# Strassen's block products in the second feed-forward stages of a two-layer decoder trunk

## The chip, the cores and the metric

The kernel runs on one core of one Trainium2 chip. The metric is device microseconds for one execution. Before the change the median of three runs is 1214.55 us (1214.17 to 1214.58).

## What is computed

A decoder trunk of two layers on a sequence of 256 rows and 1024 columns, in fp32. Each layer has a feed-forward half-step, a mixer (a state-space group beside differential attention), a cross attention into 256 memory rows, and a second feed-forward half-step. Cut to what matters here:

```python
D_MODEL = 1024; SEQ = 256; DEPTH = 2
D_FF = ((8 * D_MODEL // 3 + 127) // 128) * 128          # 2816

def rms_norm(x, gain):
    y = x * lax.rsqrt(jnp.mean(x * x, axis=-1, keepdims=True) + EPS)
    return y * gain

def swiglu(x, w_gate, w_up, w_down):
    return (jax.nn.silu(x @ w_gate) * (x @ w_up)) @ w_down

h = x
for l in range(DEPTH):
    h = h + 0.5 * swiglu(rms_norm(h, ffn1_norm[l]), ffn1_w_gate[l], ffn1_w_up[l], ffn1_w_down[l])
    h = h + hybrid_mixer(rms_norm(h, mix_norm[l]), ...)
    h = h + memory_cross_attention(rms_norm(h, xattn_norm[l]), rms_norm(mem, mem_norm[l]), ...)
    h = h + 0.5 * swiglu(rms_norm(h, ffn2_norm[l]), ffn2_w_gate[l], ffn2_w_up[l], ffn2_w_down[l])
out = rms_norm(h, final_norm)
```

## The kernel before

**Products in three parts.** Every large product is done on operands that are split in two: a high part, rounded to a shorter format by a copy on ACT (tiles whi, xh, gT), and a low part, the rest, by a subtraction on DVE (wlo, xl). One 128 x 128 by 128 x 512 block product is three matmuls: high by high, high by low, low by high.

**Units.** Weights come as units of 128 x 1024 fp32 (512 KB). stream_plan lists all of them in the order in which TensorE uses them. A unit of kind "A" belongs to a projection: it holds two blocks of 128 contraction rows by 512 columns, and with two row tiles t (128 rows of the sequence each) it feeds 2 x 2 x 3 = 12 matmuls into two product banks (tile mm). A unit of kind "B" belongs to a down projection: 128 contraction rows by 1024 columns, also 12 matmuls, into accumulators (tile acc).

**A feed-forward stage.** The 2816 inner columns are cut into NCH = 11 chunks of 256. A chunk's projection is 512 columns wide (256 of the gate, 256 of the up matrix), four units, 48 matmuls (method project). When a row tile's bank is done, ACT applies Silu to the gate half (tile sg), DVE multiplies by the up half (tile g), TensorE transposes the product (tile tp), and ACT and DVE split it (tile gT). Two chunks later (LAG = 2) its two down units follow, 24 matmuls. The last two chunks' four down units are done at the end, row tile by row tile, so that the next stage's x can be prepared meanwhile (methods blocks and prep). prep adds the residual, transposes the new h and splits it into xh and xl; the norm's scale per row is applied after the projection (self.r), the norm's gain per column is multiplied into the weights while they are split.

**Splitting.** split_unit handles half a unit, 512 columns: a copy on ACT with the gain as scale, then on DVE

```python
            self.a.activation(hi[:, s], r[:, s], AF.Copy, scale=gc)
            self.v.scalar_tensor_tensor(lo[:, s], r[:, s], gc, hi[:, s].bitcast(F32), op0=ALU.mult, op1=ALU.subtract)
```

Units without a gain use the method split: the same copy, and a plain subtraction.

**Order.** Each engine carries out its instructions in the order in which the program writes them; the program sets that order itself. The side work (evacuations, transposes, the tables of the state-space group) is written as generators, and a model of the engines' times (class Clock) decides after which matmul each next piece is written. Weights go ahead of TensorE by a plan: need[u] is the planned time of unit u, one step (STEP, 1.28) for six matmuls, and feed splits units whose need lies at most LEAD ahead, with at most N_W = 5 units split and not yet used:

```python
            if u >= self.nfree + N_W or (u > least and self.need[u] + q * STEP / 2 > self.main + LEAD):
                break
            self.split_next()
```

with LEAD = 4.0. load_to issues the transfers from the SP queue, in plan order, some four units ahead of the split, into N_RAW = 4 buffers (tile raw). The pool s4 has 12 buffers of 4 KB a partition, used for gT among others; the tiles tA, tB, tC and tD (one buffer each) hold the state-space tables in the mixer and operands of the cross attention later.

**Tables.** ssm_tables computes, with some hundred small DVE instructions and small fp32 matmuls, what the mixer's scan needs. Layer 0's run beside layer 0's first feed-forward stage, layer 1's beside layer 0's second one.

Of the kernel before, what the change touches and what calls it, by code (L numbers as in the profile page):

```python
# [11 lines left out]
F32 = mybir.dt.float32  # L12
F32R = mybir.dt.float32r
# [32 lines left out]
START = (22.0, 34.0)  # L46


def rel_bucket(n):
# [26 lines left out]
def stream_plan():  # L76

    plan = []
    for l in range(L):
        def ffn(nm):  # L80
            for j in range(NCH):
                for kp in range(4):
                    plan.append((nm + "_gu", l, 4 * j + kp, "A", (nm, l, 2 * kp), 4 if j == 0 and len(plan) >= 4 else 1))
                if j >= LAG:
                    for f in range(2):
                        plan.append((nm + "_dn", l, 2 * (j - LAG) + f, "B", None, 1))
            for n in range(2 * (NCH - LAG), 2 * NCH):
                plan.append((nm + "_dn", l, n, "B", None, 2 * LAG))

        def chunk(nm, c, norm, skew):  # L90
# [17 lines left out]
        ffn("ffn2")  # L108
    need, at, i = [], 0.0, 0
    while i < len(plan):  # L110
        n = plan[i][5]
        need += [at + STEP * k for k in range(n)]
        at += 2 * STEP * n
        i += n
    return plan, need

# [202 lines left out]
class Trunk:  # L319
    def __init__(self, ctx, tc, io):  # L320
# [24 lines left out]
        self.raw, self.w = {}, {}  # L345
        self.stream = Task(None, 0.0)
        self.nacc = self.nmm = 0
        self.accfree = [0.0, 0.0]
# [66 lines left out]
    def split(self, hi, lo, src):  # L415
        self.a.activation(hi, src, AF.Copy)
        self.v.tensor_tensor(lo, src, hi.bitcast(F32), op=ALU.subtract)

    def rstd(self, r, ssq, n, wd):
        self.g.tensor_scalar(r, ssq, 1.0 / wd, EPS, op0=ALU.mult, op1=ALU.add)  # L420
        self.g.tensor_tensor(r, r, self.mhalf[:, 0:n], op=ALU.pow)
# [16 lines left out]
    def feed(self, least=-1):  # L438

        c = self.c  # L440
        prev, c.cur = c.cur, self.stream
        n = len(self.plan)
        while self.nsplit < 2 * n:
            u, q = divmod(self.nsplit, 2)
            if u >= self.nfree + N_W or (u > least and self.need[u] + q * STEP / 2 > self.main + LEAD):
                break
            self.split_next()
        c.cur = prev

    def split_next(self):  # L450
        u, q = divmod(self.nsplit, 2)
        self.load_to(u + 1)
        self.split_unit(u, q)
        self.nsplit += 1
        self.load_to(u + N_RAW + q)

    def load_to(self, m):
        while self.nload < min(m, len(self.plan)):
            r = self.rawp.tile([128, 1024], F32, tag="raw", name="raw")
            self.tc.nc.sync.dma_start(r, self.io["wst"][self.nload])  # L460
            self.raw[self.nload] = r
            self.nload += 1

    def split_unit(self, i, q):
        kind, gain = self.plan[i][3:5]
# [186 lines left out]
        return out  # L652


    def prep(self, t, acc, coef):
        h = self.h[t]
        t0 = []
        for n in range(2):
            s = slice(512 * n, 512 * n + 512)
            self.v.scalar_tensor_tensor(h[:, s], acc[n], coef, h[:, s], op0=ALU.mult, op1=ALU.add)  # L660
            t0.append(self.c.cur.t)
        self.acc_done()
        x = self.xt()
        for n in range(2):
            self.c.cur.t = t0[n]
            yield
            yield from self.tp_wait()
            p = self.transpose4(h, [512 * n + 128 * i for i in range(4)])
            o = [a[:, 4 * n:4 * n + 4, :].rearrange("p a b -> p (a b)") for a in x]
            self.split(o[0], o[1], p)  # L670
            self.tp_done(p)
        self.x[t] = x
        with self.c.aside():
            self.row_stat(t)
# [56 lines left out]
    def ffn(self, nm, preps, tail):  # L731
# [53 lines left out]
                    self.free_unit()  # L785
        for i in range(NCH - LAG, NCH):
            self.c.wait(*tasks[i])
        base = NCH - LAG
        return self.blocks(nm + "_dn", accs, lambda t, k: xs(base + k // 2, k % 2, t), 2 * LAG, False, True, tail)

# [651 lines left out]
    def setup(self):  # L1442
# [7 lines left out]
        self.nload = 2  # L1450
# [80 lines left out]
    def run(self):  # L1531
        c = self.c
        self.setup()
        preps = None
        prep = lambda coef: (lambda t, acc: self.prep(t, acc, coef))
# [25 lines left out]
def lay_out(a):  # L1561
# [11 lines left out]
    for l in range(L):  # L1573
# [11 lines left out]
    wst = np.concatenate([groups[s, l][n:n + 1] for s, l, n, _, _, _ in stream_plan()[0]], axis=0)  # L1585
    col = lambda v: v.reshape(-1, 128).T
    gains = np.concatenate(
        [col(f[k][l]) for l in range(L)
# [30 lines left out]
```

## Time and profile before

| | before |
|---|---|
| median of three runs | 1214.55 us (1214.17 to 1214.58) |
| the profiled execution's own time | 1216.16 us |
| its span, first to last instruction | 1214.3 us |
| granted TensorE clock, mean | 0.999 |
| busy: TensorE, DVE, ACT, POOL | 1198.7, 831.3, 701.5, 45.1 us |
| bytes read from memory | 207 MB, 171 GB/s over the span |

The profile is of one execution. PE is TensorE's matmuls, PEld its weight loads, SP the queue that issues transfers. A row of a group reads: line, engine, operation, written tile <- read tiles, shapes, count | busy us, mean ns of one | the engine's idle time just before them and what ended it. Line 227 is the helper that issues every DVE instruction, 264 every ACT one, 303 every matmul, 314 every transpose, so the tiles' names tell them apart. A row of the chain reads start, duration, engine, line and count; a row of the timeline start, duration, engine, line, operation, and in brackets the idle time before it. A row of the waits reads who waited for whom: total, times, longest. A row of the windows reads the stretch, its length, and the busy time with count of PE, PEld, DVE, ACT and POOL, then clock, DMA share and GB/s.

### The profile page before, as it was taken

The page shows a single profiled execution, that of the slowest core. Times are in us where ns is not written, and L with a number is a line of the kernel's source. Part 1 is how long each engine was busy: PE and PEld are TensorE (multiplying, and loading weights), DVE is VectorE, ACT ScalarE, POOL GpSimd, SP SyncE. Part 2 cuts the span into 40 slices and gives each one's busy share as a digit, 9 for nine tenths or more (in the row PEclk, how much of TensorE's full clock was granted, in tenths as well). Part 3 has the DMA queues.
Part 4 walks back from the last instruction along what each step waited for, and adds up shares of the span by engine and source line. Part 5 has one row for each costly group of instructions (what it writes and reads, how often), then busy time and mean ns, then how long its engine had stood idle before and what let it go on. Part 6 is the DMA issues. An engine that isn't in the chain of part 4 may idle for free.

```text
span 1214.3 us, 17886 instructions
## 1 busy us (share of the span) xinstructions
PE 1198.7 (99%) x6628; PEld 979.9 (81%) x6628; DVE 831.3 (68%) x1502; ACT 701.5 (58%) x1270; POOL 45.1 (4%) x104
## 2 busy tenths in 40 slices
PE   9999999999999999999999999999999999999997
PEld 7888878777888888887888888887678888888886
DVE  5797777497767668777665655565977675655564
ACT  6665455667767555644565554465686665644553
POOL 2100001000000010000100000000000000000000
PEclk9999999999999999999999999999999999999999
DMA  8656556544644465655656555555346445655652
GB/s 281 214 181 191 163 163 188 155 138 123 208 156 138 144 209 184 190 157 158 187 176 218 169 180 192 191 168 162 122 140 209 138 146 166 199 182 191 208 181 79
DMA packets 59975, 210.92 MB, mean 174 GB/s; under 512 B 7168, under 2 KB 8288, under 8 KB 59888
## 3 DMA queue, kind: packets, MB, share of 16 engines
q1 hardware_dynamic: 56304, 202.92, 52.2%
q0 software_dynamic: 2000, 5.24, 1.5%
q10 hardware_dynamic: 1584, 1.62, 0.5%
q8 instruction: 52, 0.85, 0.3%
q14 instruction: 35, 0.29, 0.1%
HBM read 207.00 MB, written 1.05 MB: 171 GB/s over the span
## 4 chain that ended last, share of the span: by engine, by line
PE 93%; DVE 2%; ACT 2%; DMA 1%; issue 1%; ACTq 0%; POOLq 0%; POOL 0%; DVEq 0%
PE mm L303 54%; PE acc L303 32%; PE tp L314 5%; PE tp L303 1%; DMA uq<-z 1%; DVE wlo L227 1%; DVE p L227 1%; ACT junk L264 0%; DMA h<-in_x 0%; ACT whi L264 0%; ACT z L264 0%; DVE nm L227 0%; DVE yT L227 0%; ACT yg L264 0%; ACT up L264 0%
## 5 line engine op out<-in xcount | busy, mean ns | idle before, releaser
L227 DVE SCALAR_TENSOR_TENSOR wlo<-raw,gains,whi 128x512 fp32r<-128x512 f32 x544 | 383.8, 746 | 96.9 <-ACT whi L264 92.5
L264 ACT ACTIVATE whi<-raw,gains 128x512 fp32r<-128x512 f32 x544 | 353.7, 713 | 14.2 <-DMA raw<-in_wst 7.0
L303 PE MATMUL mm<-whi,xh 128*128 128x512 f32 x896 | 356.5, 398 | 0.0
L303 PE MATMUL mm<-whi,xl 128*128 128x512 f32 x896 | 349.8, 390 | 0.0
L303 PE MATMUL mm<-wlo,xh 128*128 128x512 f32 x896 | 349.3, 390 | 0.3 <-DVE wlo L227 0.3
L303 PE MATMUL acc<-whi,gT 128*128 128x512 f32 (+1 forms) x712 | 239.7, 399 | 0.0
L303 PEld LDWEIGHTS mm<-whi,xh 128*128 128x128 f32 x896 | 168.6, 188 | 36.3 <-issue 1.3
L303 PEld LDWEIGHTS mm<-whi,xl 128*128 128x128 f32 x896 | 168.5, 188 | 35.6
L303 PEld LDWEIGHTS mm<-wlo,xh 128*128 128x128 f32 x896 | 168.8, 188 | 33.0 <-DVE wlo L227 0.6
L227 DVE TENSOR_TENSOR wlo<-raw,whi 128x512 fp32r<-128x512 f32 x224 | 147.3, 686 | 37.3 <-ACT whi L264 35.7
L264 ACT ACTIVATE whi<-raw 128x512 fp32r<-128x512 f32 x224 | 130.6, 624 | 59.8 <-DMA raw<-in_wst 42.7
L303 PEld LDWEIGHTS acc<-whi,gT 128*128 128x128 f32 x712 | 133.3, 188 | 25.8
L264 ACT ACTIVATE sg<-mm,rstd 128x256 f32<-128x256 f32 x88 | 41.8, 475 | 190.3 <-PE mm L303 190.1
L303 PE MATMUL acc<-wlo,gT 128*128 128x512 f32 (+1 forms) x356 | 138.2, 388 | 0.0
L227 DVE SCALAR_TENSOR_TENSOR g<-mm,rstd,sg 128x256 f32<-128x256 f32 x88 | 42.4, 482 | 129.0 <-ACT sg L264 128.5
L303 PE MATMUL mm<-whi,mem 128*128 128x512 f32 x256 | 92.6, 410 | 0.0
L303 PEld LDWEIGHTS acc<-wlo,gT 128*128 128x128 f32 x356 | 67.2, 189 | 11.0
L264 ACT ACTIVATE xh<-tp 128x512 fp32r<-128x512 f32 x40 | 23.9, 598 | 77.8 <-PE tp L314 77.8
L303 PEld LDWEIGHTS mm<-whi,mem 128*128 128x128 f32 x256 | 48.1, 188 | 11.5 <-issue 1.3
L303 PE MATMUL mm<-wlo,mem 128*128 128x512 f32 x128 | 51.0, 398 | 3.5 <-DVE wlo L227 3.5
L227 DVE TENSOR_TENSOR xl<-tp,xh 128x512 fp32r<-128x512 f32 x40 | 27.6, 689 | 31.7 <-ACT xh L264 31.7
L264 ACT ACTIVATE gT<-tp 128x512 fp32r<-128x512 f32 x44 | 26.3, 599 | 36.7 <-PE tp L314 36.7
(214 smaller groups left out, 1093.6 us busy)
## 6 DMA issues: line engine op xcount, KB each, us to landing
raw<-in_wst SPq DMA_DIRECT2D x382, 512.0 KB, 4.2
raw<-in_wst SPq DMA_DIRECT2D x4, 256.0 KB, 5.1
mem<-in_mem POOLq DMA_DIRECT2D x2, 512.0 KB, 6.3
uq<-z ACTq DMA_DIRECT2D x8, 128.0 KB, 4.8
bglu<-in_b_glu POOLq DMA_DIRECT2D x2, 512.0 KB, 3.8
h<-in_x SPq DMA_DIRECT2D x3, 256.0 KB, 5.7
bc<-in_s5b POOLq DMA_DIRECT2D x2, 256.0 KB, 3.0
bc<-in_s5c POOLq DMA_DIRECT2D x2, 256.0 KB, 3.1
```

The lines of the kernel that those rows point to most:

```text
L227: r = getattr(self.e, name)(*a, **k)
L264: r = self.e.activation(out, in_, func, **k)
L303: r = self.e.matmul(out, lhsT, rhs, **k)
L314: r = self.e.transpose(out, in_, ident)
```

## The change

In both second feed-forward stages six of the eleven chunks, the pairs (3,4), (6,7) and (9,10), are computed as 2 x 2 block matrices: x in blocks of 128 rows by 512 columns, the two chunks' weights in blocks of 512 by 512 (two units each). Seven block products of 12 matmuls replace the eight block products of two projections. The form used is

```python
PAIR = (
    ("Q3", (1, 1), "X", "X", None),
    ("Q1", (0, 0), "P", "P", None),
    ("Q7", (1, 0), "Y", "X", "Y"),
    ("Q6", None, None, "X", "P"),
    ("Q2", (0, 1), "Q", "Q", None),
    ("Q5", None, None, "Y", "P"),
    ("Q4", None, None, "X", "Q"),
)
SECOND = (("P", 0, (), ()), ("P", 1, (), ()), ("P", 2, (), ()), ("S", 3, (0, 1, 2), ()), ("P", 5, (), ()),
          ("S", 6, (3, 4, 5), ()), ("P", 8, (), ()), ("S", 9, (6, 7), (8,)))
```

(the fields of PAIR: product, weight block that is loaded, tile it is loaded to, tile that is the operand, tile that is first added to the operand in place). So each pair loads its four blocks, eight units, once; X and Y live in tB and tD, P and Q in s4. In SECOND, "P" is a chunk as before and "S" a pair; the first tuple lists the chunks whose down units are spread between the seven products of the pair, the second those that follow it. The down units of chunks 0 to 8 thus move into and behind the pairs.

The split of a unit in these two stages is done whole, after the sum where there is one:

```diff
+    def split_whole(self, i):
+        hi = self.hip.tile([128, 1024], F32R, tag="hi", name="whi")
+        lo = self.lop.tile([128, 1024], F32R, tag="lo", name="wlo")
...
+        if kind == "S":
+            pair, u, _, operand, add = op
+            r = self.blk[pair, operand, u]
+            if add is not None:
+                self.v.tensor_tensor(r, r, self.blk[pair, add, u], op=ALU.add)
+        else:
+            r = self.raw.pop(i)
+        self.split(hi, lo, r)
```

A block product is two units, for one row block of x or a combination of its blocks:

```diff
+        def block(ps, name):
+            xh, xl = E[name]
+            for u in range(2):
+                w = self.unit(nm + "_gu")
+                for i in range(2):
+                    self.tick(w[2 + i])
...
+                    self.p.matmul(ps, xh[:, k, :], w[0][:, s], start=k == 0, stop=False)
+                    self.p.matmul(ps, xh[:, k, :], w[1][:, s], start=False, stop=False)
+                    self.p.matmul(ps, xl[:, k, :], w[0][:, s], start=False, stop=k == 3)
+                self.free_unit()
```

Its result is combined on DVE with those of other products (ACT copies Q3, Q1 and Q7 out of their banks; sums runs after Q6, c11 after Q2, c12 after Q5, c21 after Q4), and then goes through Silu, gate, transposes and split as before:

```diff
+            def sums():
+                yield st["q1"]
+                v.tensor_tensor(u2, ps, q1, op=ALU.add)
+                self.mm_done()
+                yield st["q7"]
+                v.tensor_tensor(u3, u3, u2, op=ALU.add)
+                yield st["q3"]
+                v.tensor_tensor(q3, q3, u2, op=ALU.subtract)
+
+            def c11():
+                yield st["u"]
+                v.tensor_tensor(q1, ps, q1, op=ALU.add)
+                self.mm_done()
+                yield
+                swiglu(q1, q1, 0)
+
+            def c12():
+                yield st["u"]
+                v.scalar_tensor_tensor(u2, ps, -1.0, u3, op0=ALU.mult, op1=ALU.subtract)
+                v.tensor_tensor(q3, q3, ps, op=ALU.subtract)
+                self.mm_done()
+                yield
+                swiglu(u2, u2, 1)
+                swiglu(q3, q3, 0)
```

The method combos, started after chunk 0, makes the four combinations of x's blocks that Q3, Q7, Q6 and Q5 need: two 1024-wide sums of xh and xl, four 512-wide combinations, four 512-wide splits into tA and tC.

Since a sum of weight blocks and a combination of x's blocks must go with the plain weights, the norm's gain is multiplied into x here: prep ahead of the second stage calls split_gain, which per half row does four 128-wide copies on ACT, each with its column gain as scale, and four 128-wide multiply-subtracts on DVE, instead of one 512-wide of each.

Last, the tables of layer 1 are moved, since the second stage of layer 0 now uses tA to tD:

```diff
         for l in range(L):
+            if l:
+                tb = {}
+                tables = [c.spawn(self.ssm_tables(l, tb), c.now + 12.0)]
             preps = self.ffn("ffn1", preps, prep(0.5))
             preps = self.mixer(l, preps, tb, tables, prep(1.0))
-            preps = self.cross(l, preps, prep(1.0))
-            if l < L - 1:
-                tb = {}
-                tables = [c.spawn(self.ssm_tables(l + 1, tb), c.now + 10.0)]
+            preps = self.cross(l, preps, prep(1.0, ("ffn2", l)))
...
-            preps = self.ffn("ffn2", preps, prep(0.5) if l < L - 1 else (lambda t, acc: self.final(t, acc, 0.5)))
+            preps = self.ffn_second("ffn2", preps, prep(0.5) if l < L - 1 else (lambda t, acc: self.final(t, acc, 0.5)))
```

In the plan a unit of a pair counts one step (six matmuls) instead of two.

More of the change, by code (lines that the diff above doesn't have):

```diff
@@ L46, with second_items @@
 START = (22.0, 34.0)
+SECOND = (("P", 0, (), ()), ("P", 1, (), ()), ("P", 2, (), ()), ("S", 3, (0, 1, 2), ()), ("P", 5, (), ()), ("S", 6, (3, 4, 5), ()), ("P", 8, (), ()), ("S", 9, (6, 7), (8,)))
+PAIR = (
[7 more added lines that the diff above has]
+)
+def second_items():
+    for kind, j, inner, after in SECOND:
+        down = [("D", i, f) for i in inner for f in range(2)]
+        if kind == "P":
+            yield "P", j, 0
+            yield from down
+        else:
+            for k in range(7):
+                yield "S", j, k
+                n = (len(down) * (k + 1)) // 7 - (len(down) * k) // 7
+                first = (len(down) * k) // 7
+                yield from down[first:first + n]
+        for i in after:
+            for f in range(2):
+                yield "D", i, f
 def rel_bucket(n):
@@ L88, in ffn, with second @@
                 plan.append((nm + "_dn", l, n, "B", None, 2 * LAG))
+        def second(nm):
+            for kind, j, k in second_items():
+                if kind == "P":
+                    for kp in range(4):
+                        plan.append((nm + "_gu", l, 4 * j + kp, "A", None, 4 if j == 0 else 1))
+                elif kind == "D":
+                    plan.append((nm + "_dn", l, 2 * j + k, "B", None, 1))
+                else:
+                    _, block, to, operand, add = PAIR[k]
+                    for u in range(2):
+                        n = None if block is None else 4 * (j + block[0]) + 2 * block[1] + u
+                        plan.append((nm + "_gu", l, n, "S", ((l, j), u, to, operand, add), 1))
+            for n in range(2 * (NCH - LAG), 2 * NCH):
+                plan.append((nm + "_dn", l, n, "B", None, 2 * LAG))
         def chunk(nm, c, norm, skew):
@@ L417, in split, with split_gain @@
         self.v.tensor_tensor(lo, src, hi.bitcast(F32), op=ALU.subtract)
+    def split_gain(self, x, n, src, nm, l):
+        g0 = l * NGAIN + GOFF[nm] + 4 * n
+        gc = [self.gains[:, g0 + i:g0 + i + 1] for i in range(4)]
+        blk = [slice(128 * i, 128 * i + 128) for i in range(4)]
+        o = [a[:, 4 * n:4 * n + 4, :].rearrange("p a b -> p (a b)") for a in x]
+        for g, b in zip(gc, blk):
+            self.copy(o[0][:, b], src[:, b], scale=g)
+        t = self.c.cur.t
+        self.c.cur.t -= 0.6
+        for g, b in zip(gc, blk):
+            self.v.scalar_tensor_tensor(o[1][:, b], src[:, b], g, o[0][:, b].bitcast(F32), op0=ALU.mult, op1=ALU.subtract)
+        self.c.cur.t = max(self.c.cur.t, t)
     def rstd(self, r, ssq, n, wd):
@@ L652, in blocks, with prep @@
         return out
-    def prep(self, t, acc, coef):
+    def prep(self, t, acc, coef, gain=None):
         h = self.h[t]
@@ L668, in prep @@
             p = self.transpose4(h, [512 * n + 128 * i for i in range(4)])
-            o = [a[:, 4 * n:4 * n + 4, :].rearrange("p a b -> p (a b)") for a in x]
-            self.split(o[0], o[1], p)
+            if gain is not None:
+                self.split_gain(x, n, p, *gain)
+            else:
+                o = [a[:, 4 * n:4 * n + 4, :].rearrange("p a b -> p (a b)") for a in x]
+                self.split(o[0], o[1], p)
             self.tp_done(p)
@@ L787, in ffn, with combos @@
             self.c.wait(*tasks[i])
+        base = NCH - LAG
+        return self.blocks(nm + "_dn", accs, lambda t, k: xs(base + k // 2, k % 2, t), 2 * LAG, False, True, tail)
+    def combos(self, E):
+        v = self.v
+        xf = []
+        for t in range(2):
+            f = self.s4t([128, 1024], name="xf")
+            v.tensor_tensor(f, self.x[t][0].rearrange("p a b -> p (a b)").bitcast(F32),
+                            self.x[t][1].rearrange("p a b -> p (a b)").bitcast(F32), op=ALU.add)
+            xf.append(f)
+            yield
+        a11, a12, a21, a22 = (xf[t][:, 512 * k:512 * k + 512] for t in range(2) for k in range(2))
+        e = [self.s4t([128, 2, 512], name="ef") for _ in range(2)]
+        e4, e2, e3, e1 = (x[:, i, :] for x in e for i in range(2))
+        v.tensor_tensor(e4, a11, a21, op=ALU.subtract)
+        yield
+        v.tensor_tensor(e2, a22, a21, op=ALU.subtract)
+        yield
+        v.scalar_tensor_tensor(e3, e4, -1.0, a22, op0=ALU.mult, op1=ALU.subtract)
+        yield
+        v.tensor_tensor(e1, a12, e3, op=ALU.add)
+        yield
+        hi = self.tab.tile([128, 4, 4, 128], F32R, tag="tA", name="eh")
+        lo = self.tab.tile([128, 4, 4, 128], F32R, tag="tC", name="el")
+        for i, (nm, f) in enumerate((("Q3", e1), ("Q7", e4), ("Q6", e3), ("Q5", e2))):
+            h, g = hi[:, i], lo[:, i]
+            self.split(h.rearrange("p a b -> p (a b)"), g.rearrange("p a b -> p (a b)"), f)
+            E[nm] = (h, g)
+            yield
+        half = lambda t, k: tuple(x[:, 4 * k:4 * k + 4, :] for x in self.x[t])
+        E.update(Q1=half(0, 0), Q2=half(0, 1), Q4=half(1, 1))
```

156 lines of the change are left out of this document (142 added, 14 removed).

## The prediction

> **What bounds the kernel now.** I read the page's head first, then the chain, the waits, and one stretch of the second feed-forward stage.
>
> ```profile
> span 1214.3 us, 17886 instructions
> ...
> PE 1198.7 (99%) x6628; PEld 979.9 (81%) x6628; DVE 831.3 (68%) x1502; ACT 701.5 (58%) x1270; POOL 45.1 (4%) x104
> ...
> PEclk9999999999999999999999999999999999999999
> ...
> PE 93%; DVE 2%; ACT 2%; DMA 1%; issue 1%; ACTq 0%; POOLq 0%; POOL 0%; DVEq 0%
> ```
>
> TensorE is busy 99% of the span at its full granted clock, and 93% of the chain is its own work. DVE has a third of its time over.
>
> The waits of TensorE and of DVE:
>
> ```profile
> PE mm L303 <- DVE wlo L227: 3.8, 5, 1.4
> ...
> DVE wlo L227 <- ACT whi L264: 128.3, 92, 4.8
> ```
>
> TensorE hardly waits for a weight (3.8 us in all), though DVE waits 128.3 us for ACT's high parts. Those waits cost nothing, because DVE works ahead of TensorE.
>
> The chain, piece by piece, in layer 1's first feed-forward stage (the second has the same pattern), and the same stretch as a window (PE, PEld, DVE, ACT busy):
>
> ```profile
> 660.47 10.88 PE mm L303 x48
> 671.35 0.22 PE tp L314 x2
> 671.57 1.39 PE acc L303 x6
> 672.96 0.22 PE tp L314 x2
> 673.18 4.11 PE acc L303 x18
> 677.30 10.88 PE mm L303 x48
> ...
> 660.47:694.12 33.65, 33.65 (x153) 27.69 (x153) 19.48 (x31) 17.51 (x31) 0.00 (x0) 1.00 0.56 187
> ```
>
> A chunk takes 677.30 - 660.47 = 16.83 us: 48 projection matmuls, 24 down matmuls, four transposes. One matmul takes 10.88/48 = 0.2267 us, a transpose 0.11 us. TensorE is the bound, with DVE at 19.48/33.65 = 58%.
>
> **The change, part by part.** Times are per pair of chunks.
>
> *Matmuls.* A pair needs 96 projection matmuls before (2 x 48) and 7 x 12 = 84 after. Twelve fewer are 2.72 us; six pairs give 16.3 us, the most that the change can bring. With six down units before as after, a pair takes 2 x 16.83 + 24 x 0.2267 = 39.1 us now; TensorE's own work becomes 156 x 0.2267 + 8 x 0.11 = 36.3 us. The last pair has four down units: 33.66 us before.
>
> *Block sums.* This is the term that decides. Four of the seven products (Q7, Q6, Q5, Q4) read a weight block that is first summed, so 8 of 14 units run through split_whole as: DVE adds in place, ACT copies the sum to the high part, DVE subtracts the high part. The two DVE instructions are neighbours in DVE's queue, and the second needs ACT's copy of the first. The rows that price this:
>
> ```profile
> L227 DVE TENSOR_TENSOR p<-p 128x1024 f32<-128x1024 f32 x4 | 4.9, 1220 | 0.1
> L264 ACT ACTIVATE up<-uq 128x1024 f32<-128x1024 f32 x2 | 2.1, 1056 | 5.5 <-DMA uq<-z 5.5
> ...
> 482.98 1.22 DVE L227 TENSOR_TENSOR ang<-ang,rnd 128x1024 f32<-128x1024 f32 x1
> 484.12 1.41 DVE L227 SCALAR_TENSOR_TENSOR wlo<-raw,gains,whi 128x512 fp32r<-128x512 f32 x2
> ...
> 484.23 1.06 ACT L264 ACTIVATE rot<-ang 128x1024 f32<-128x1024 f32 x1 [1.77 <-DVE ang L227]
> ```
>
> A 1024-wide sum lasts 1.22 us, and an independent DVE successor starts 1.14 us after it (484.12 - 482.98). ACT starts 0.03 us after the sum ends (482.98 + 1.22 = 484.20, then 484.23) and takes 1.06.
>
> How the queues keep their order is seen at a chunk's end, in the second feed-forward stage of layer 1 (chain, ACT, DVE):
>
> ```profile
> 1094.63 10.88 PE mm L303 x48
> ...
> 1104.19 0.47 ACT L264 ACTIVATE sg<-mm,rstd 128x256 f32<-128x256 f32 x1 [5.42 <-PE mm L303]
> 1104.56 0.62 ACT L264 ACTIVATE whi<-raw 128x512 fp32r<-128x512 f32 x1
> ...
> 1104.69 0.48 DVE L227 SCALAR_TENSOR_TENSOR g<-mm,rstd,sg 128x256 f32<-128x256 f32 x1 [5.20 <-ACT sg L264]
> 1105.21 0.69 DVE L227 TENSOR_TENSOR wlo<-raw,whi 128x512 fp32r<-128x512 f32 x1
> 1106.06 0.48 DVE L227 SCALAR_TENSOR_TENSOR g<-mm,rstd,sg 128x256 f32<-128x256 f32 x1 [0.15 <-ACT sg L264]
> 1106.67 0.75 DVE L227 SCALAR_TENSOR_TENSOR wlo<-raw,gains,whi 128x512 fp32r<-128x512 f32 x1
> 1108.01 0.69 DVE L227 TENSOR_TENSOR gT<-tp,gT 128x512 fp32r<-128x512 f32 x1 [0.59 <-ACT gT L264]
> 1108.62 4.73 DVE L227 SCALAR_TENSOR_TENSOR wlo<-raw,gains,whi 128x512 fp32r<-128x512 f32 x7
> ```
>
> ACT stood 5.42 us behind sg with the weight copy next in its queue; DVE stood 5.20 us behind g with the weight work next in its own. Nothing overtakes. DVE takes up again 0.03 us after ACT ends (1104.66, 1104.69). So a summed unit occupies DVE's queue for 1.22 + 0.03 + 1.06 + 0.03 + 1.14 = **3.48 us**, of which DVE works 2.36; TensorE uses the unit up in 6 x 0.2267 = 1.36.
>
> *Where DVE starts.* Let T0 be the end of the projection before the pair (here 1094.63 + 10.88 = 1105.51). The weights ready then reach some 4 us ahead (LEAD). g and gT still hold DVE; the row at 1108.62 shows it free for later weights 3.1 us after T0. I take 3.2 for the first summed unit, Q7's. Ends: 1.2 (right after g at 1106.06) and 4.5 (one more 1.14 in front).
>
> *DVE's queue from there to the pair's last down unit.* Nearest rows for its 512-wide and 256-wide work:
>
> ```profile
> L227 DVE TENSOR_TENSOR wlo<-raw,whi 128x512 fp32r<-128x512 f32 x224 | 147.3, 686 | 37.3 <-ACT whi L264 35.7
> L227 DVE SCALAR_TENSOR_TENSOR g<-mm,rstd,sg 128x256 f32<-128x256 f32 x88 | 42.4, 482 | 129.0 <-ACT sg L264 128.5
> ```
>
> Eight summed units 27.84; Q2's two plain units 2.28; five down units 5.70; the three dependent sums after Q6 3 x 0.69 = 2.07; c11's sum and gate 0.69 + 0.48 = 1.17; c12's two sums 1.3. Together 40.4 us. The last down unit is ready at T0 + 43.6, and its other 11 matmuls end at T0 + 46.1. That is 39.1 -> 46.1, **+7.0 us** for each of the first two pairs of a layer, not -2.7. In between come chunks 5 and 8, whose 10.88 us of matmuls need only 4 x 1.14 us of weight work, so each pair starts with its lead restored and repays nothing. The third pair has two down units fewer: 46.1 - 2 x 1.14 = 43.8 against 33.66, **+10.1 us**. Two layers: 2 x (7.0 + 7.0 + 10.1) = **+48.2 us**. With the ends above (-2 and +1.3 at the start; -1 if gate work is fully covered; +2 if the waits for Silu or for a product bank add 0.5 at four places), a pair moves by -3 to +3.3, the whole from +30 to +68.
>
> *Combinations of x* (combos): two 1024-wide and eight 512-wide instructions on DVE, 2 x 1.14 + 8 x 0.61 = 7.2 us a layer, in chunks 1 and 2. DVE's 14 us of idle time in the quoted window hide it: taken at 0; without that cover 7.2 us a layer, and 2 as upper end.
>
> *Gain on x* (split_gain): per half, four 128-wide instructions on each engine instead of one 512-wide.
>
> ```profile
> L227 DVE SCALAR_TENSOR_TENSOR sb<-sb,sums 128x128 f32<-128x128 f32 x8 | 2.8, 351 | 0.3
> L264 ACT ACTIVATE junk<-on 128x128 bf16<-128x128 f32 x16 | 5.0, 311 | 0.5
> ```
>
> Four are 1.24 on ACT, and the last 0.35 on DVE follows: 1.6 against 1.3 before (a 512-wide copy at 0.62, as at 1104.56, and a subtraction at 0.69). Row tile 0's 24 projection matmuls (5.4 us) cover row tile 1's preparation: 0; uncovered 0.3 a half, 2.4 us in all.
>
> *Whole-unit splits* shorten the queues (one 1.14 for two of 0.67 on DVE). TensorE gains nothing from it: 0. Each block then waits for the whole unit, inside the lead.
>
> *Transfers.* A pair loads eight blocks as before. X and Y have one buffer each, so SP holds the next pair's X until Q4's last subtraction.
>
> ```profile
> raw<-in_wst SPq DMA_DIRECT2D x382, 512.0 KB, 4.2
> SPq L460 <- DVE wlo L227: 881.4, 321, 8.2
> ```
>
> SP waits like this already. Q4's units are split at about T0 + 41, both X units land 8.4 us later at the worst, and the next pair begins at T0 + 57: 0.
>
> *SSM tables* of layer 1 move from layer 0's second stage into layer 1's first, with their POOL transfers, DVE work and fp32 matmuls.
>
> ```profile
> L287 POOL DMA_DIRECT2D bc<-in_s5b x2: 544/546/548, 15.2 to 431.6; - x2
> L227 DVE TENSOR_TENSOR dd<-dc,cst x4: 406/412/418, 181.8 to 583.1; 16x256 f32<-16x256 f32 x4
> ```
>
> They take 583.1 - 431.6 = 152 us. The stage lasts 11 x 16.83 = 185 and they start 12 us into it, ending 20 us before the mixer. The quoted window shows DVE 42% idle there: 0. If the cover went, the mixer would wait out the difference.
>
> **The rivals.** *A (other side, faster): the sums do not stall DVE.* If a summed unit cost only DVE's own 1.14 + 1.14 = 2.28, the queue falls by 8 x 1.2 = 9.6 us: the last down unit is ready at T0 + 34, just when TensorE gets there (36.3 - 2.7). Two pairs gain 2.7, the third ends at 34.2 and loses 0.5: 2 x (-5.4 + 0.5) = -10, time 1205. The lead of 4 us and DVE's 42% idle time speak for it, the strict order in the rows above against. It decides below 3.48 - 48.2/48 = 2.5 us a summed unit. *A2: everything hidden,* -16.3, time 1198; the third pair's DVE work, as just counted, speaks against it.
>
> *B: TensorE's clock falls in the stalls.* The clock row shows full speed throughout, with 1.4 us as the longest wait for a weight; I expect gaps of 3.48 - 1.36 = 2.1 us, longer than any shown. Were matmuls twice as long in these stretches, a pair's would need 72.6 us instead of 46.1, the third (30.9 us of work) 61.7 instead of 43.8: 2 x (26.5 + 26.5 + 17.9) = +142 on top, time about 1404. The Trainium skill, "TensorE: Matmul & The Clock Gate", section "What's actually happening", says the array falls to half clock after about 3.4 us without work. By that rule gaps of 2.1 us keep the clock, as the trace's full clock across shorter gaps bears out so far; no run here shows a longer one.
>
> *C: block transfers come late* through SP's order. At SP's longest wait, 8.2 us, at the four joints between pairs: +33 on top, time 1295. The 8 us of slack worked out above speak against it.
>
> **How the numbers follow.** The profiled execution took 1216.16 us (span 1214.3), 1.6 over the median of 1214.55. On it the sum gives 1264.4; on the median 1214.55 + 48.2 = 1262.8. My forecast has 0.84, with its own range 1244 to 1284; A 0.06, A2 0.01, B 0.02, C 0.04, and 0.03 for a summed unit near 2.5 us, where nothing changes. The range 1236 to 1288 leaves out A, A2, B and the case of no change (0.12), most of C (0.03) and tails of the forecast that I put at 0.05. Slower by over 0.2% (about what a measurement here tells from no change): 0.84 + 0.02 + 0.04 = 0.90; same 0.03; faster 0.07.
>
> **What would show it.** In the profile after: 72 fewer 512-wide matmuls; 48 in-place 1024-wide sums on DVE, each followed by about 1.1 us of idle time ahead of the subtraction, put down to ACT; TensorE waiting some 60 us for wlo, in gaps near 2 us, nearly all in six stretches; the granted clock still full; a pair near 46 us and chunks 5 and 8 unchanged at their 10.88. I am wrong if DVE's idle time before those subtractions is small (A), the clock row dips (B), or ACT's copies wait for transfers (C).

## The result, and the profile after

| | before | after |
|---|---|---|
| median | 1214.55 us | 1294.84 us (1293.85 to 1295.94, four runs) |
| ratio after / before | | 1.0658 [1.0645, 1.0671] |
| profiled execution, its span | 1216.16, 1214.3 us | 1295.58, 1293.8 us |
| granted TensorE clock, mean | 0.999 | 0.984 |

The change costs 80.3 us. The prediction had +48.2 and an upper end of 1288. So the sign and, as will be seen, the main mechanism came out, and the size did not. One execution of the kernel with both sums first, shown below, took 6757.91 us against 1234.74 to 1235.95 of its others, and is left out of that kernel's time.

The page's head after, with the same rows as before (line 274 is now the helper of DVE's instructions, 311 of ACT's, 334 of POOL's, 350 of the matmuls, 361 of the transposes):

```profile
span 1293.8 us, 17730 instructions
...
PE 1217.8 (94%) x6556; PEld 970.5 (75%) x6556; DVE 947.8 (73%) x1540; ACT 725.9 (56%) x1224; POOL 45.1 (3%) x104
...
PEclk9999999999999999998899999999999999999989
...
PE 74%; DVE 12%; ACT 6%; issue 6%; DMA 2%; ACTq 0%; SPq 0%; POOLq 0%; DVEq 0%; POOL 0%
```

The 72 matmuls are gone (6628 to 6556), but TensorE's share of the chain fell from 93% to 74%, and what it lost went to DVE, ACT and issue. The clock row has dips near 600 us and near the end of the span: the third pair of each layer. The row shows tenths over 32 us; shorter dips come below.

The chain of waits of the changed kernel gives a clock for each part (start, duration, engine, line, count). The first rows are layer 0's second feed-forward stage, the last four layer 1's:

```profile
447.39 9.59 PE mm L350 x42
...
502.47 2.83 PE acc L350 x11
...
511.23 6.87 PE mm L350 x30
...
572.32 6.85 PE mm L350 x30
...
620.38 5.25 PE mm L350 x12
...
636.22 7.38 PE acc L350 x30
...
1084.72 9.59 PE mm L350 x42
...
1148.86 6.84 PE mm L350 x30
...
1210.31 6.85 PE mm L350 x30
...
1274.36 5.38 PE acc L350 x21
```

The projection before the first pair ends at 447.39 + 9.59 = 456.98, chunk 5's at 511.23 + 6.87 = 518.10, chunk 8's at 572.32 + 6.85 = 579.17, and the end blocks begin at 636.22. Before the change a pair with the chunk behind it took 3 x 16.83 = 50.5 us, and the last three steps (chunks 9 and 10 and the down units up to the end blocks) 33.65 + 5.44 and four transposes, 0.44: 39.5. (These are chunks without the work on layer 1's tables, which has moved.) So:

| stretch | before | predicted | after, layer 0 | after, layer 1 |
|---|---|---|---|---|
| pair (3,4) and chunk 5 | 50.5 | +7.0 | 61.1 (+10.6) | 61.4 (+10.9) |
| pair (6,7) and chunk 8 | 50.5 | +7.0 | 61.1 (+10.6) | 61.5 (+11.0) |
| pair (9,10) to the end blocks | 39.5 | +10.1 | 57.1 (+17.6) | 57.2 (+17.7) |

These six add up to 78.4 of the 79.5 us by which the span grew. On balance next to nothing was lost in the mixers, the cross attention or the first stages.

**The summed unit.** The timeline of DVE at the start of the first pair (start, duration, engine, line, operation, in brackets the idle time before it and what ended it):

```profile
461.34 1.22 DVE L274 TENSOR_TENSOR blkX<-blkX,blkY 128x1024 f32<-128x1024 f32 x1
463.74 1.23 DVE L274 TENSOR_TENSOR wlo<-blkX,whi 128x1024 fp32r<-128x1024 f32 x1 [1.19 <-ACT whi L311]
464.88 1.22 DVE L274 TENSOR_TENSOR blkX<-blkX,blkY 128x1024 f32<-128x1024 f32 x1
```

From one sum to the next it is 464.88 - 461.34 = 3.54 us, and in the middle DVE stands still for 1.19 while ACT copies. The groups of DVE (busy us, mean ns | idle before, and who ended it) say how often:

```profile
L274 DVE TENSOR_TENSOR wlo<-blkX,whi 128x1024 fp32r<-128x1024 f32 x48 | 58.4, 1225 | 44.0 <-ACT whi L311 44.0
...
L274 DVE TENSOR_TENSOR wlo<-blkY,whi 128x1024 fp32r<-128x1024 f32 x12 | 14.7, 1226 | 14.5 <-ACT whi L311 14.5
```

The first group holds 36 summed units and Q3's 12 plain ones, the second 12 summed ones: 58.5 us of idle time over 48 sums, 1.2 each.

**The waits of TensorE** (total, times, longest):

```profile
PE mm L350 <- DVE wlo L274: 26.5, 37, 1.4
PE mm L350 <- ACT whi L311: 16.6, 22, 1.5
PE mm L350 <- DVE qs L274: 16.0, 6, 6.8
```

The first two are weights that come late, 43.1 us in many short waits. The third the prediction had only in its upper end, at 0.5 us a place: TensorE waits for a product bank that DVE has not emptied, up to 6.8 us at once.

**The third pair.** DVE just before that wait, then TensorE through it:

```profile
610.68 1.22 DVE L274 TENSOR_TENSOR blkX<-blkX,blkQ 128x1024 f32<-128x1024 f32 x1
613.11 1.23 DVE L274 TENSOR_TENSOR wlo<-blkX,whi 128x1024 fp32r<-128x1024 f32 x1 [1.21 <-ACT whi L311]
...
614.85 1.22 DVE L274 TENSOR_TENSOR blkX<-blkX,blkQ 128x1024 f32<-128x1024 f32 x1
617.27 1.23 DVE L274 TENSOR_TENSOR wlo<-blkX,whi 128x1024 fp32r<-128x1024 f32 x1 [1.20 <-ACT whi L311]
618.41 1.22 DVE L274 TENSOR_TENSOR wlo<-raw,whi 128x1024 fp32r<-128x1024 f32 x1
619.55 0.68 DVE L274 TENSOR_TENSOR qs<-mm,qs 128x512 f32<-128x512 f32 x1
```

```profile
590.75 0.49 PE L350 MATMUL mm<-wlo,eh 128*128 128x512 f32 x1 [0.76 <-DVE wlo L274]
...
593.03 0.50 PE L350 MATMUL mm<-whi,eh 128*128 128x512 f32 x1 [0.86 <-ACT whi L311]
594.29 0.62 PE L350 MATMUL mm<-wlo,eh 128*128 128x512 f32 x1 [0.76 <-DVE wlo L274]
594.71 0.63 PE L350 MATMUL mm<-whi,el 128*128 128x512 f32 x1
...
620.38 0.77 PE L350 MATMUL mm<-whi,xh 128*128 128x512 f32 x1 [6.77 <-DVE qs L274]
620.95 0.63 PE L350 MATMUL mm<-wlo,xh 128*128 128x512 f32 x1
621.37 0.63 PE L350 MATMUL mm<-whi,xl 128*128 128x512 f32 x1
```

The instruction at 619.55 is c11, the one that empties Q2's bank. Q4 needs a bank to write into. But c11 stands in DVE's queue behind both of Q4's sums, both of its subtractions, the last of the sums after Q6 and a down unit, so TensorE, which had Q4's first weights at 613.11 + 1.23 = 614.3, starts Q4 at 620.38. And then it starts slowly: matmuls follow each other at 621.37 - 620.95 = 0.42 us instead of 0.2267.

That slow spacing appears elsewhere as well: from 594.29 on, the matmuls are 0.42 us apart (594.71 - 594.29), with no wait longer than 0.86 us in the 5 us before it. Windows of 16 us show one more place, in the first pair, and none in the second (stretch, length, busy PE, PEld, DVE, ACT, POOL, clock, DMA share, GB/s):

```profile
488.00:504.00 16.00, 11.45 (x39) 8.05 (x39) 12.39 (x15) 8.16 (x10) 0.00 (x0) 0.89 0.17 41
...
552.00:568.00 16.00, 12.53 (x51) 8.89 (x51) 12.68 (x15) 7.29 (x10) 0.00 (x0) 1.00 0.31 108
```

In layer 1 it is four places: 1137 and 1198 us, in the first two pairs, and 1233 and 1256 in the third. So the clock fell seven times, two of them in the long waits for the bank.

### The profile page after: what moved, and what is told of

Its sections match the earlier page's. It is cut to its first block, busy times and chain, and to the rows that moved or that the text cites. A ratio compares the mean times of both kernels' runs of the same rounds, so it can differ in the third digit from the quotient of the medians.

```text
span 1293.8 us, 17730 instructions
## 1 busy us (share of the span) xinstructions
PE 1217.8 (94%) x6556; PEld 970.5 (75%) x6556; DVE 947.8 (73%) x1540; ACT 725.9 (56%) x1224; POOL 45.1 (3%) x104
## 4 chain that ended last, share of the span: by engine, by line
PE 74%; DVE 12%; ACT 6%; issue 6%; DMA 2%; ACTq 0%; SPq 0%; POOLq 0%; DVEq 0%; POOL 0%
PE mm L350 43%; PE acc L350 25%; DVE wlo L274 5%; ACT whi L311 5%; PE tp L361 4%; DVE blkX L274 3%; PE tp L350 2%; DVE qs L274 2%; DVE blkY L274 1%; DMA uq<-z 1%; DVE p L274 1%; DMA raw<-in_wst 0%; ACT gT L311 0%; ACT qs L311 0%; DVE gT L274 0%
## 5 line engine op out<-in xcount | busy, mean ns | idle before, releaser
L350 PE MATMUL mm<-whi,xh 128*128 128x512 f32 x776 | 314.4, 405 | 19.3 <-DVE qs L274 16.0
L274 DVE SCALAR_TENSOR_TENSOR wlo<-raw,gains,whi 128x512 fp32r<-128x512 f32 x368 | 263.1, 747 | 92.7 <-ACT whi L311 91.2
L350 PE MATMUL mm<-wlo,xh 128*128 128x512 f32 x776 | 305.9, 394 | 5.9 <-DVE wlo L274 5.9
L350 PE MATMUL mm<-whi,xl 128*128 128x512 f32 x776 | 305.7, 394 | 0.0
L311 ACT ACTIVATE whi<-raw,gains 128x512 fp32r<-128x512 f32 x368 | 240.6, 713 | 13.1 <-issue 5.3
L274 DVE TENSOR_TENSOR wlo<-raw,whi 128x512 fp32r<-128x512 f32 (+1 forms) x220 | 191.4, 891 | 20.8 <-ACT whi L311 19.9
L311 ACT ACTIVATE whi<-raw 128x512 fp32r<-128x512 f32 (+1 forms) x220 | 165.4, 786 | 35.6 <-DMA raw<-in_wst 15.5
L311 ACT ACTIVATE whi<-blkX 128x1024 fp32r<-128x1024 f32 x48 | 50.3, 1057 | 90.8 <-DVE blkX L274 90.8
L274 DVE TENSOR_TENSOR wlo<-blkX,whi 128x1024 fp32r<-128x1024 f32 x48 | 58.4, 1225 | 44.0 <-ACT whi L311 44.0
L350 PE MATMUL mm<-wlo,eh 128*128 128x512 f32 x96 | 41.9, 436 | 16.8 <-DVE wlo L274 16.8
```

Source lines behind the costliest of these rows:

```text
L274: r = getattr(self.e, name)(*a, **k)
L311: r = self.e.activation(out, in_, func, **k)
L350: r = self.e.matmul(out, lhsT, rhs, **k)
```

## The experiments

Each kernel is the changed one with the edit shown, and each ratio is to the kernel before, timed on the same chip. Where two kernels are set side by side, it is by their ratios, rounded to whole microseconds.

### Both sums first: is it the stall?

In the changed kernel a block's two units run sum, copy, subtraction, sum, copy, subtraction. Here DVE does both sums, then both subtractions; the instructions and TensorE's order are the same. (load_to sees to it that the second unit's block has been requested when it is summed.)

```diff
-            if add is not None:
-                self.v.tensor_tensor(r, r, self.blk[pair, add, u], op=ALU.add)
+            if add is not None and u == 0:
+                self.load_to(i + 2)
+                for k in range(2):
+                    b = self.blk[pair, operand, k]
+                    self.v.tensor_tensor(b, b, self.blk[pair, add, k], op=ALU.add)
```

> Both block sums of a product are written ahead of its two splits (sum 0, sum 1, subtraction 0, subtraction 1); the same instructions, TensorE's order is unchanged. If the stall between a sum and its own subtraction is what costs (theory S), a summed product holds DVE for 4 x 1.14 = 4.6 us instead of 2 x 3.48 = 7.0; a pair's queue loses 9.4 us, the first two pairs of a layer become bound by TensorE again (span from projection end to projection end 61.1 -> about 52 us), the third loses as much, and the time falls by 45 to 60 us, to about 1240. If DVE's amount of work is the limit (theory W), the time stays within 1% of 1294.8, since the work is the same. If the fallen clock costs most by itself (theory C), the time falls by under 20 us.

Measured: 1235.22 us, ratio 1.0168 [1.0151, 1.0185], some 59 us below the changed kernel. DVE's timeline of this kernel at the first summed block:

```profile
460.64 2.35 DVE L274 TENSOR_TENSOR blkX<-blkX,blkY 128x1024 f32<-128x1024 f32 x2
463.04 2.36 DVE L274 TENSOR_TENSOR wlo<-blkX,whi 128x1024 fp32r<-128x1024 f32 x2
```

ACT copies the first unit while DVE sums the second. The pair of units takes 465.40 - 460.64 = 4.76 us, 2.38 a unit, and the subtractions follow the sums at once. Three quarters of the loss was the order of four instructions, with what hung on it: TensorE's waits for qs fell too, from 16.0 to 11.2 us.

### The sums left out: is the sums' own work covered?

The addition is removed, so the four products use unsummed blocks; the rest of the work stays.

```diff
-            if add is not None:
-                self.v.tensor_tensor(r, r, self.blk[pair, add, u], op=ALU.add)
```

> The in-place sums of the weight blocks are left out (four products are computed from unsummed blocks); everything else stays. DVE loses 48 x 1.14 = 55 us of work and all stalls between sum and subtraction. Theories S and W both: down to 1205 to 1225, by S at most some 15 us below the kernel with both sums first, by W 70 us or more below it. Theory C: above 1260, with the clock row still at 8 in places.

Measured: 1200.17 us, ratio 0.9879 [0.9859, 0.9899], some 35 us below the kernel with both sums first. That lies between the two expectations, at most 15 and at least 70. The 48 sums are some 48 x 1.2 = 58 us of DVE work, and 35 of them come out of the time: for so much of that work DVE has no idle time at the place where it stands. Without the sums the form's fewer matmuls bring some 14 of the 16.3 us that the prediction called the most possible.

### Plain chunks: what do the other edits cost?

All eleven chunks are done as before; the gain on x, the whole-unit splits, the combinations of x and the moved tables stay.

```diff
-SECOND = (("P", 0, (), ()), ... ("S", 9, (6, 7), (8,)))
+SECOND = tuple(("P", j, (j - LAG,) if j >= LAG else (), ()) for j in range(NCH))
```

> No pairs: all eleven chunks of the second stages as plain projections with the down units two chunks behind, as before the change; the gain on x, the whole-unit splits, the combinations of x (now unused) and the moved tables stay. I put all of these at 0: 1214.5 within 3 us. If they carry a cost of their own (combos up to 14 us, the moved tables up to some 10), the time is above 1220.

Measured: 1215.12 us, ratio 1.0003 [0.9993, 1.0012]. Together they cost nothing that can be measured, as each was taken.

### c11 in its place: what is the product bank's wait worth?

c11's sum is written as soon as Q2's matmuls and the sums after Q6 are, instead of at a point that the planner picks.

```diff
-                yield st["u"]
-                v.tensor_tensor(q1, ps, q1, op=ALU.add)
-                self.mm_done()
                 yield
                 swiglu(q1, q1, 0)
...
             elif name == "Q2":
+                c.wait(st["u"])
+                v.tensor_tensor(q1, ps, q1, op=ALU.add)
+                self.mm_done()
                 st["c11"] = c.spawn(c11())
```

> c11's sum, which frees Q2's product bank, is written right after Q2's matmuls instead of when the time model lets it come up. In the third pair of a layer TensorE waited 6.8 us for that bank and then ran 12 matmuls at half rate (5.25 us instead of 2.72). If that wait is a cost of its own beside the stalls, 6 us a layer go: 1294.8 -> about 1283. If DVE's queue is the limit wherever the sum stands (the wait only moves), the time stays within 3 us of 1294.8.

Measured: 1288.87 us, ratio 1.0612 [1.0594, 1.0629], some 6 us less than the changed kernel and not 12. The waits of TensorE in this kernel:

```profile
PE mm L350 <- DVE wlo L274: 28.0, 40, 1.4
PE mm L350 <- ACT whi L311: 21.6, 26, 2.1
...
PE mm L350 <- DVE qs L274: 2.5, 4, 0.6
```

The bank's wait fell by 13.5 us (16.0 to 2.5), but waits for weights rose by 1.5 and 5.0. DVE was the late engine anyhow: an earlier c11 takes its place ahead of Q4's weights, whose first sum then starts 33.8 us after chunk 8's end instead of 31.5. A wait's length is not its price where the engine behind it is the bound.

### Useless matmuls in the wait: what does the clock cost?

24 matmuls into an unused transpose bank are issued ahead of Q4 of the pairs (9,10), so that TensorE works through the long wait.

```diff
+            if name == "Q4" and j == 9:
+                d = self.tp.tile([128, 512], F32, tag="tp", name="tp")
+                xh = E[name][0]
+                for _ in range(24):
+                    self.p.e.matmul(d, xh[:, 0, :], xh.rearrange("p a b -> p (a b)"), start=True, stop=True)
             block(ps, name)
```

> The changed kernel with 24 matmuls without use (into a transposes' bank) ahead of Q4's matmuls in the third pair, 24 x 0.227 = 5.4 us inside TensorE's wait of 6.8 us there. If the clock falls because TensorE stands idle in that wait, Q4's 12 matmuls take 2.7 us instead of 5.25 and the time falls by about 5 us, to 1290, with everything else unchanged. If the clock falls for another reason, 1294.8 within 2 us.

Measured: 1289.97 us, ratio 1.062 [1.0604, 1.0636], some 5 us less than the changed kernel, with 48 more matmuls. TensorE's timeline in this kernel:

```profile
612.37 5.60 PE L993 MATMUL tp<-xh 128*128 128x512 f32 x24
...
619.60 0.39 PE L350 MATMUL mm<-wlo,xh 128*128 128x512 f32 x1
619.83 0.40 PE L350 MATMUL mm<-whi,xl 128*128 128x512 f32 x1
```

The matmuls after the wait follow each other at the full 0.23 us. So the fallen clock behind the two long waits was worth about 5 us of the 80, 2.5 in each layer, which is what Q4's 5.25 instead of 2.72 us said. The other dips, at 594 us for one, are in this kernel too (594.10); no run took them away alone.

### Both edits together

Both sums first, and c11 in its place.

> Both sums of a product first, and c11's sum right after Q2's matmuls. In the kernel with both sums first TensorE still waits 11.2 us for qs in all, two of the waits 4.3 us long, with 12 matmuls at half rate behind each (5.14 us). If these waits are a cost beside DVE's work, 1235.6 falls by 6 to 14 us, to 1222 to 1230; if DVE's work fills the third pair anyway, it stays within 3 us.

Measured: 1230.08 us, ratio 1.0129 [1.0112, 1.0146]. The chain in layer 0 of this kernel, and two windows of the third pair (length; PE, PEld, DVE, ACT and POOL busy):

```profile
446.86 10.93 PE mm L350 x48
...
501.03 6.83 PE mm L350 x30
...
552.53 6.85 PE mm L350 x30
...
603.79 7.42 PE acc L350 x30
```

```profile
560.00:575.00 15.00, 14.14 (x62) 11.06 (x61) 14.42 (x14) 10.66 (x13) 0.00 (x0) 1.00 0.27 94
575.00:590.00 15.00, 12.14 (x50) 9.04 (x49) 14.28 (x16) 6.50 (x8) 0.00 (x0) 0.99 0.24 72
```

The first pair with chunk 5 now takes 507.86 - 457.79 = 50.1 us (before: 50.5), the second 559.38 - 507.86 = 51.5, and the third to the end blocks 603.79 - 559.38 = 44.4 (before: 39.5). In the third pair DVE is busy 14.42 and 14.28 of 15 us: 96%. No stall between a sum and its subtraction is left there. From 559.38 to 603.79 DVE works 40.0 us, which is more than the whole stretch took before the change, and TensorE still waits up to 1.8 us for Q4's weights.

### The sums on POOL

POOL is busy 3% of the span. Here it does the sums.

```diff
-                self.v.tensor_tensor(r, r, self.blk[pair, add, u], op=ALU.add)
+                self.g.tensor_tensor(r, r, self.blk[pair, add, u], op=ALU.add)
```

> The in-place block sums are done by POOL instead of DVE, in the same places of the program; POOL's queue is empty there, so a sum starts as soon as its blocks are there. DVE loses 48 x 1.14 us of work and the stall. If POOL does a 128x1024 sum in under some 3 us and does not slow DVE, the time comes near that of the kernel without sums: 1200 to 1215. If POOL is late (over 4 us a sum, 8 in 36 us) or slows DVE's own instructions, the wait moves to ACT's copy behind POOL's sum, and the time lies between 1220 and 1290.

> Sums on POOL and c11's sum written right after Q2's matmuls. If the sums on POOL alone free DVE enough, c11 comes in time anyway, and this is within 4 us of them alone; if the third pair's bank wait stays there, this is 4 to 12 us faster.

Measured: 1255.74 us, ratio 1.0336 [1.032, 1.0351]; with c11 in its place too, 1256.11 us, 1.0338 [1.0322, 1.0353], no different. That is 39 us better than the sums on DVE one by one, and 20 us worse than on DVE two by two. The groups of POOL and of DVE in the first of them:

```profile
L334 POOL TENSOR_TENSOR blkY<-blkY,blkP 128x1024 f32<-128x1024 f32 x12 | 40.2, 3374 | 0.0
```

```profile
L274 DVE TENSOR_TENSOR wlo<-blkQ,whi 128x1024 fp32r<-128x1024 f32 x12 | 40.4, 3407 | 0.0
```

A sum takes POOL about 3.4 us, and while it runs, DVE's subtraction of the same width, 1.22 us otherwise, takes 3.4 us as well. The work left DVE's queue and came back as slower work.

### Where does the form pay?

Two pairs a layer instead of three, (4,5) and (8,9), each with four chunks' down units between its products instead of three or two; both edits from above are in.

```diff
+SECOND = (("P", 0, (), ()), ("P", 1, (), ()), ("P", 2, (), ()), ("P", 3, (), ()), ("S", 4, (0, 1, 2, 3), ()),
+          ("P", 6, (), ()), ("P", 7, (), ()), ("S", 8, (4, 5, 6, 7), ()), ("P", 10, (), (8,)))
```

> Sums first and c11 early as in the run before, and the pairs spread out: two a layer, (4,5) and (8,9), with eight down units inside each (chunks 0 to 3, 4 to 7), two plain chunks between them, chunk 10 plain at the end. Inside a pair TensorE has 84 + 96 = 180 matmuls, 41.7 us with transposes; DVE has 16 x 1.14 of summed units, 2 + 4 plain... in all 22 units and 8 sums at 1.14, 34.2 us, and some 7 us of 512-wide work: 41, no more than TensorE. If DVE's share inside the pairs is what is left of the loss, each pair gives its 2.7 us: 1214.6 - 4 x 2.7 = 1204, within 4. If something else of the pairs costs (product banks, transfers of blocks, clock), 1214 or more.

Measured: 1211.40 us, ratio 0.9969 [0.9957, 0.998]. A window over both pairs of layer 0:

```profile
440.00:620.00 180.00, 178.06 (x808) 144.96 (x807) 143.56 (x161) 100.58 (x131) 5.21 (x12) 1.00 0.55 191
```

TensorE is at 99% again and DVE at 80%. With more matmuls of down units to a summed block, DVE's work fits beside them. The expectation was some 7 us lower.

Three pairs with both edits, the third also given a third chunk of down units, so that none is left behind it:

```diff
-          ("S", 9, (6, 7), (8,)))
+          ("S", 9, (6, 7, 8), ()))
```

> Sums first and c11 early, three pairs as in the change, but chunk 8's down units inside the third pair instead of behind it, so that it has six. If the third pair's shortage of matmuls beside DVE's work is what makes it the dearest, 3 to 8 us a layer come back: 1230 -> about 1220. But the last two chunks' products are then followed at once by their own down units: their evacuation (some 4 us a layer) has no cover any more; if that decides, 1230 within 3.

Measured: 1233.27 us, ratio 1.0149 [1.0136, 1.0163], no better than with chunk 8's units behind the pair (1.0129). TensorE's waits have a new row:

```profile
PE tp L361 <- DVE qs L274: 6.2, 4, 2.9
```

Behind the pair, chunk 8's down units had covered the evacuation of its last products. Now the transposes wait for these products.

Then more lead for the two-pair kernel: LEAD = 5.2 instead of 4.0, first everywhere, then for the second feed-forward stages alone.

```diff
-LEAD = 4.0
+LEAD = 5.2
```

> The same with the plan's lead at 5.2 us instead of 4.0 in the whole kernel (the five buffers of split units allow no more). If DVE is late at the start of a pair, the longer lead gives up to 1.2 us a pair, 5 us in all, below the run beside it; if the pairs are bound by TensorE, within 2 us of it; evacuations queued behind more splits could cost 1 to 5 us.

Measured: 1215.99 us, ratio 1.0011 [1.0002, 1.002]. TensorE's waits:

```profile
PE tp L361 <- DVE yT L274: 4.8, 3, 2.0
```

TensorE's transposes in the mixer now wait for small DVE instructions such as yT. That weight work stands ahead of them in DVE's queue is the likely reason; the next kernel, with 4.0 in the mixer again, has no such row.

```diff
-            if u >= self.nfree + N_W or (u > least and self.need[u] + q * STEP / 2 > self.main + LEAD):
+            if u >= self.nfree + N_W or (u > least and self.need[u] + q * STEP / 2 > self.main + (5.2 if self.plan[u][0].startswith("ffn2") else LEAD)):
```

> The kernel with two pairs a layer (1211.4), with the lead of 5.2 us for the units of the second feed-forward stages alone and 4.0 elsewhere. In the run with 5.2 everywhere TensorE waited only 1.5 us for weights in projections, against 6.4, but waits of the mixer's transposes for DVE appeared (yT, vl, prob: 9.8 us). If the lead of the pairs and the mixer's waits are separate, this gives 1211.4 - 4 to 6 = 1206 to 1208, faster than before by about 0.6%. If the lead in the pairs only moves evacuations back, 1211 within 2.

Measured: 1207.86 us, ratio 0.9942 [0.9928, 0.9956]: the fastest here, 0.6% below the kernel before. Four pairs save 4 x 2.72 = 10.9 us of matmuls, and 7 arrive.

## Why the prediction was right, and where it was wrong

**Right: what decides.** The summed unit was priced at 3.48 us of DVE's queue and took 3.54; DVE's idle time before each subtraction was to be about 1.1 us and is 1.2. With this one stall taken away the time fell by some 59 of 80.3 us, so it was shown by a run and not only argued. The third pair is the dearest, as said. The edits taken at 0 (gain on x, whole-unit splits, combinations, tables) are at 0: 1.0003 [0.9993, 1.0012].

**Wrong: the size of a pair's loss.** The forecast failed at two steps: in the first two pairs, at DVE's start and at the claim that the chunk behind a pair repays nothing; in the third, at a wait for a product bank, which was left out of the sum, allowed 0.5 us at its upper end, and was 6.8 (of which some 3 us a layer came back when it was taken away). +7.0 for each of the first two pairs was +10.6 to +11.0. In layer 0's first pair the missing 3.6 us, within rounding, are these:

- *DVE's start*, taken at T0 + 3.2, was 461.34 - 456.98 = 4.36, near the end of the bound (4.5): 1.2 us.
- *The queue's length*, 40.4 us from there, held within 1 us: the last down unit's matmuls begin at 502.47, T0 + 45.5 instead of T0 + 43.6, of which 1.2 is the start and 0.7 the queue. With the matmuls behind it (2.83 instead of 2.5) the pair ends at T0 + 48.3 instead of T0 + 46.1.
- *"Chunks 5 and 8 repay nothing, unchanged at 10.88"* failed. From the end of the pair's last down unit (502.47 + 2.83 = 505.30) to chunk 5's end at 518.10 it is 12.8 us, where the projection with its four transposes takes 10.88 + 4 x 0.11 = 11.3. TensorE's timeline shows where: four transposes of the pair come first, from 505.14 on, then six matmuls of chunk 5, and then 0.62 us of waiting until 507.75, since c21's sum (507.01 + 0.68) still held a product bank. The pair's last evacuation runs into the chunk behind it: 1.5 us.

**Wrong: the product banks.** The step "+2 if the waits for Silu or for a product bank add 0.5 at four places" gave an upper bound from nothing but smallness. TensorE's waits for qs are 16.0 us, the longest 6.8. The sum of c11 was counted in the queue's length, but its *place* in the queue was not looked at. The planner put c11 behind 8.9 us of other work (610.68 to 619.55), most of it Q4's weights. In the third pair the wait of 6.77 and the 2.5 of slow matmuls behind it lie where the 7.5 us beyond the forecast were lost. They are not its price, though: with c11 in its place 13.5 us of waiting went and some 6 us came back, since c11 moved forward puts weights back. Layer 0's third pair then takes 631.54 - (571.45 + 6.85) = 53.2 instead of 57.1 us. The other 3.6 us beyond the forecast are not separated; DVE's first sum is 1.2 us late here too (583.52), and ahead of the end blocks TensorE waits 0.55 and 0.69 us for the pair's last gated product.

**Wrong: TensorE's waits for weights.** They were to be some 60 us for wlo, in gaps near 2 us. They are 43.1 us, for wlo and whi, in gaps of at most 1.5: in a summed unit TensorE stops twice, once for each part.

**Rival A (the sums do not stall DVE, 1205)** fell as the forecast, and it was mispriced too. The kernel with both sums first meets its condition, 2.38 us a summed unit, and stands at 1235.22. A pair was to gain 2.7, the third to lose 0.5. With c11 in its place as well, the first pair gains 0.4, the second loses 1.0 and the third 4.9. The prediction's threshold, "below 2.5 us a summed unit", is therefore also wrong: at 2.38 the change still loses 1.7%. DVE's queue was added up to end just when TensorE gets there, and a sum that comes out even leaves nothing over for an evacuation, a gate or a Silu that comes at the wrong moment; where DVE is 96% busy, as in the third pair, it is the bound.

**Rival B (the clock falls in the stalls)** was held at 0.02, with the argument that gaps of 2.1 us, one by one, leave the clock alone. It happened in part: behind the two long waits it cost about 5 us, by the experiment with useless matmuls, and not the 142 of the rival. In five other places the clock fell too, at little cost where it can be compared: pair (6,7) of layer 0, at full clock, lost 10.6 us, and the three of the first two pairs with a fall 10.6 to 11.0, for DVE was the late engine. The step that failed is that single gaps were judged. At 594.29 us no gap had been above 0.9 us. But in the 3.5 us before (590.75 to 594.29) TensorE had stood for 0.86 + 0.76 us, and the gap of 0.76 lay just ahead; it worked about half the time.

The Trainium skill, "TensorE: Matmul & The Clock Gate", section "What's actually happening", has the array fall to half clock after an idle window of about 3.4 us. By that rule the clock falls at 620 us, after 6.77 us of waiting, and the trace agrees there; at 594 us the trace differs, since no idle stretch of that length preceded, and the measurement decides.

**Rival C (late blocks)** is out. None of DVE's waits is for a transfer, and ACT's waits before the copies of the X blocks are all for DVE:

```profile
L311 ACT ACTIVATE whi<-blkX 128x1024 fp32r<-128x1024 f32 x48 | 50.3, 1057 | 90.8 <-DVE blkX L274 90.8
```

That the time came out at C's 1295 is chance: the place and the mechanism are others.

**What stays open.** The 80.3 us were split by experiments into some 59 for the stall and, from there, a further 5 (ratio 1.0168 to 1.0129) for c11's place; the remaining 16 are the third pairs, where DVE is full (4.9 in layer 0, 4.1 in layer 1), and smaller pieces that no run separated. Why the two-pair kernel gets 7 and not 10.9 us was not settled either.

## What to carry to other kernels

When one engine hands a tile to another and needs it back for its next instruction, the other's time is added to its own: 1.2 us per unit here, some 59 us in all. Put a second tile's first step in between before any other remedy. Count the work of an engine stretch by stretch, and where it comes within a few per cent of the stretch, take it as the bound and look at the *place* of every evacuation in its queue. And spread such work: two pairs with much other work between their products beat three with little.

## What the runs showed of the hardware

- **Two engines on one memory.** A DVE instruction that reads two SBUF tiles took 3.41 us beside a POOL sum of the same width, instead of 1.22. One with a source in PSUM kept its time. The timelines of DVE and of POOL in the kernel with the sums on POOL:

```profile
569.69 0.48 DVE L274 SCALAR_TENSOR_TENSOR z<-mm,rstd,z 128x256 f32<-128x256 f32 x1
```

```profile
477.45 6.71 POOL L334 TENSOR_TENSOR blkX<-blkX,blkQ 128x1024 f32<-128x1024 f32 x2
...
566.15 5.73 POOL L334 TENSOR_TENSOR blkX<-blkX,blkY 128x1024 f32<-128x1024 f32 x2 [25.76 <-DMA blkY<-in_wst]
```

  POOL's two sums from 477.45 on take 3.35 us each, and DVE's two subtractions beside them (478.49 to 485.24) are of the group shown with that experiment, at 3.407 us. At 569.69 a POOL sum is under way too, and DVE's instruction on a product bank takes 0.48, what the gate of this size took before the change (482 ns).

  The Trainium skill, "GPSIMD Engine Reference", section "1. Specifications", says that POOL shares its SBUF interfaces with DVE, with contention for DVE instructions with two SBUF inputs. The runs agree, and give the size.
- **The clock falls without a long gap.** In five places of the changed kernel (492, 594, 1137, 1198 and 1233 us) matmuls fell to 0.42 us apart with no wait above 1.5 us in the 5 us before, after some 3.5 us in which TensorE worked about half the time (1.61 of 3.50 from 488.5 to 492). Such a stretch is not enough, however: from 549.6 to 553.1, in pair (6,7), it also worked 1.61 of 3.50, and the clock stayed full. Q4's twelve matmuls after the long wait ran at half rate too, 5.25 us instead of 2.72. What decides was not tried.
